# Exponential biases and softmax division computed on ScalarE in place of VectorE and GpSimd

## The chip, the core and the metric

The kernel runs on one core of a Trainium2 chip. The metric is device time in microseconds (us) of one execution. Five engines work side by side, each through its own list of instructions in a fixed order: TensorE (PE, with its weight loads as PEld), VectorE (DVE), ScalarE (ACT), GpSimd (POOL) and SyncE (SP), which issues the DMAs. An instruction waits, by semaphores, for what it reads and for the buffer that it writes, and everything behind it in the same list waits with it.

## The reference, cut to what matters

```python
proj = x @ w_in + b_in                       # x is layer-normed; 1024 x 1024 by 1024 x 3912
ya = spatial_gating(gelu(a_u), gelu(a_v), ...)
yb = chunk_band_attention(bq, bk, bv, b_rel)     # own chunk and 8 chunks before it
yc = dsa_attention(cq, ck, cv, iq, ik, iw, t5)   # top 256 keys by an indexer, then attention
ym = memory_attention(mq, km, vm)                # 256 memory tokens
mixed = concat([ya*silu(a_g), yb*silu(bg), yc*silu(cg), ym*silu(mg)])
out = layer_norm(ALPHA * x + (mixed @ w_out + b_out), ln_g, ln_b)

# in each of the three attentions, for every head and row:
p = softmax(s)          # exp(s - max(s)) / sum(exp(s - max(s)))
o = p @ v
```

All is float32. There are 1024 positions, and 4 heads of 64 in each group.

## The kernel before

Positions stand in 8 blocks of 128 (`rb`). Heads go in pairs (`odd` = 0, 1), so each attention has two pairs and 16 items (pair by block): M (memory, items of two blocks each), B (band) and C (top-k). Projections are three-part matmuls of 128x512 (`acc`), high and low halves of both operands.

An item of attention goes through these steps, which `mix_of` (B, C) and `mix_of_m` (M) write out. **scores**: PE makes `qk` in PSUM; DVE adds the bias and takes the row maximum (`mx`, or `nb` by a reduction in M); from it the bias of the exponential is made, `nb` = shift - max; ACT computes `sc` = exp(s + nb) and its row sum `rsum`. **turn**: `sc` is transposed to `pT`, for M and B by POOL (two float16 halves, lines 543 and 544) and a DMA transpose, for C by PE, ACT and DVE (`spread`). **values**: PE makes `pv`; `normalized` adds its three parts on DVE (`o`), takes the reciprocal `ri` of `rsum`, and multiplies `o` by `ri`. **close**: PE transposes `o` (bank `pt`), and DVE multiplies it by the gate into `mix`, which goes to DRAM or straight into the output projection.

The order of the work is written out by `weave`: parts of attention items alternate with pieces of projections ("fillers" on PE). A second filler is the search for the top-k threshold of C, bit by bit over 31 rounds: ACT counts three blocks (`jka`), DVE three others (`jk`), then DVE settles the bit in three small instructions (`bit`, `thr`, `cand`). It runs beside M and B; after it `masks` turns the scores into 0 or -1e30, and C reads them. The final order on each engine is set when the program is built, by a planner with costs of its own, so a changed instruction also moves others.

In `normalized`, `(V if kt in O_V else G)` sends the multiplication to DVE for `kt` 2 to 5 (B and C, 32 times) and to POOL for `kt` 6 (M, 16 times). `nb` is made by DVE, 8 times in M and 32 times in B and C.

Of the kernel before, what the change touches and what calls it, by code (L numbers as in the profile page):

```python
# [11 lines left out]
F32 = mybir.dt.float32  # L12
# [6 lines left out]
AF = mybir.ActivationFunctionType  # L19
ALU = mybir.AluOpType  # L20
# [4 lines left out]
P = 128  # L25
# [8 lines left out]
PSHIFT = 14.0 * math.log(2.0)  # L34
# [5 lines left out]
C0_FIRST, LATE = (0, 1, 6, 7, 5), "17 16 15 14 04 13 03 12 02 11 10"  # L40
HR = 2
WH = (0, 0)
O_V = (2, 3, 4, 5)
MHB = 2
LAG_O = 14
OB, LB = 400, 0
# [32 lines left out]
def tile_trunk(ctx, tc, x, mem, ln_in_g, ln_in_b, w_in, b_in, a_ln_g, a_ln_b, a_ws, a_bs,  # L79
               b_rel_rev, t5_table, w_mem, w_out, b_out, ln_g, ln_b, bucket1h, out):  # L80
    nc = tc.nc
    G, SP = nc.gpsimd, nc.sync
# [20 lines left out]
    PE, V, S = Engine(nc.tensor), Engine(nc.vector), Engine(nc.scalar)  # L103
# [9 lines left out]
    cp = ctx.enter_context(tc.tile_pool(name="cp", bufs=1))  # L113
# [6 lines left out]
    make_identity(nc, ident)  # L120
    mhalf = cp.tile([P, 1], F32, name="mhalf")
    V.memset(mhalf, -0.5)
    one = cp.tile([P, 1], BF16, name="one")
    S.activation(one, mhalf, AF.Copy, scale=-2.0)

# [11 lines left out]
    bias = cp.tile([P, 31], F32, name="bias")  # L137
# [33 lines left out]
    def small(shape, name, bufs=3):  # L171
        return gp.tile(list(shape), F32, tag=name, bufs=bufs, name=name)
# [81 lines left out]
    def two_heads(q, k, pieces):  # L254

        last = None
        for accs, c, n, qs, ks in pieces:
            for t, (x, y) in enumerate(((q[0], k[0]), (q[1], k[0]), (q[0], k[1]))):  # L260
                for odd in range(2):
                    rows = slice(64 * odd, 64 * odd + 64)
                    ins = PE.matmul(accs[odd][:, c:c + n], x[rows, qs:qs + P], y[rows, ks:ks + n],
                                    start=(t == 0), stop=(t == 2))
                    if last is not None:
                        tc.add_manual_dep(ins.ins, last.name, mybir.DependencyInfo(
                            mybir.DependencyClass.NoSync, mybir.DependencyReason.DATA), reason="in turn")
                    last = ins.ins

    def two_banks():  # L270
        return bank("qk"), bank("pt", "qk")
# [264 lines left out]
    def turned(sc, n):  # L536

        row, nb = sc.bitcast(F16), n // P  # L540
        both = 4 * n <= 2048
        high, rest = row[:, 2 * n:3 * n], row[:, 3 * n:4 * n] if both else row[:, :n]
        G.tensor_scalar(high, sc[:, :n], 1.0, 0.0, ALU.mult, ALU.add)  # L543
        G.tensor_sub(rest, sc[:, :n], high)  # L544
        t = gp.tile([P, 10, P], F16, tag="pT", bufs=TB, name="pT")
        if both:
            SP.dma_start_transpose(out=t[:, :2 * nb, :], in_=row[:, 2 * n:4 * n])
        else:
            SP.dma_start_transpose(out=t[:, :nb, :], in_=high)
            SP.dma_start_transpose(out=t[:, nb:2 * nb, :], in_=rest)  # L550
        return [t[:, j] for j in range(nb)], [t[:, nb + j] for j in range(nb)]
# [9 lines left out]
    def normalized(pv, rsum, kt):  # L561

        ri = small([P, 2], "ri")
        V.reciprocal(ri, rsum)
        o = small([P, 2, 64], "o", 2)
        done.append(V.tensor_reduce(o, pv[:, :384].rearrange("p (h t d) -> p h d t", h=2, t=3), AX.X, ALU.add).ins)
        (V if kt in O_V else G).tensor_mul(o, o, ri.unsqueeze(2).to_broadcast([P, 2, 64]))
        return o

    def gated(o, gate, dst):  # L570
# [97 lines left out]
    def mix_of_m(pair, rbs, q):  # L668

        d = {}  # L670

        def scores():
            accs = two_banks()
            two_heads(q, kmem[pair], [(accs, 256 * r, 256, rb * P, 0) for r, rb in enumerate(rbs)])
            nb = small([P, 2, 2], "nb2")
            for odd in range(2):
                V.tensor_reduce(nb[:, odd], accs[odd].rearrange("p (r n) -> p r n", r=2), AX.X, ALU.max)
            V.tensor_scalar(nb, nb, -0.125, PSHIFT, ALU.mult, ALU.add)
            for r in range(2):
                d["rsum", r] = small([P, 2], "rsum", 5)  # L680
                sc = gp.tile([P, 1024], F32, tag="S", bufs=SB, name="sc")
                for odd in range(2):
                    S.activation(sc[:, odd * 256:odd * 256 + 256], accs[odd][:, 256 * r:256 * r + 256], AF.Exp,
                                 bias=nb[:, odd, r:r + 1], scale=0.125, accum_out=d["rsum", r][:, odd:odd + 1])
                d["p", r] = turned(sc, 512)

        def values(r):
            ph, pl = d["p", r]
            pv = bank(("pv", "pt")[r], "pv")
            for odd in range(2):  # L690
                for i in range(2):
                    pv_mm(pv, odd, ph[2 * odd + i], pl[2 * odd + i], v3m[pair][:, i, odd], i == 0, i == 1)
            d["o", r] = normalized(pv, d["rsum", r], 6)

        def close():
            for r, rb in enumerate(rbs):
                t = small([P, P], "mix", 2)
                gated(d["o", r], gate_of(6 + pair, rb), t)
                store_mix(6 + pair, rb, t)

        return Item(scores, [], [lambda: values(0), lambda: values(1)], close)

    def mix_of(kt, rb, kb0, st, near, far_of, last):

        by_dma = kt < 4
        q, k, v3 = st
        nk = rb + 1 - kb0
        n = nk * P
        nfar = max(0, n - 256)
        chunks = list(range(0, nk, 4))  # L710
        d = {}

        def scores():
            d["rsum"] = small([P, 2], "rsum", 5)
            d["sc"] = [gp.tile([P, 1024], F32, tag="S", bufs=SB, name="sc") for _ in range(2)]
            mx = small([P, 2, 4], "mx")
            nr = [near(odd) for odd in range(2)]
            nmx = [0, 0]
            pieces = [(a, b) for a, b in pieces_of(n)]
            for group in [pieces] if by_dma else [[piece] for piece in pieces]:  # L720
                banks = [two_banks() if by_dma else (bank("qk"), bank("qk")) for _ in group]
                two_heads(q, k, [(accs, 0, b - a, rb * P, kb0 * P + a) for accs, (a, b) in zip(banks, group)])
                for (a, b), accs, odd in [(*x, odd) for x in zip(group, banks) for odd in range(2)]:
                    for lo, hi in ((a, min(b, nfar)), (max(a, nfar), b)):
                        if lo >= hi:
                            continue
                        other = far_of(lo, hi) if hi <= nfar else nr[odd][:, 256 - n + lo:256 - n + hi]
                        i = nmx[odd]
                        V.tensor_tensor_reduce(d["sc"][odd][:, lo:hi], accs[odd][:, lo - a:hi - a], other, 0.125,
                                               mx[:, odd, i - 1:i] if i else -3e38, ALU.add, ALU.max, mx[:, odd, i:i + 1])  # L730
                        nmx[odd] += 1
            nb = small([P, 2], "nb")
            V.tensor_scalar(nb, mx[:, :, nmx[0] - 1], -1.0, PSHIFT, ALU.mult, ALU.add)
            for odd in range(2):
                sc = d["sc"][odd]
                S.activation(sc[:, :n], sc[:, :n], AF.Exp, bias=nb[:, odd:odd + 1], accum_out=d["rsum"][:, odd:odd + 1])
                if by_dma:
                    d["p", odd] = turned(sc, n)

        def turn(odd, c):  # L740
            sc = d["sc"][odd]
            m = min(4, nk - c)
            pt = bank("pt")
            for j in range(m):
                PE.transpose(pt[:, j * P:(j + 1) * P], sc[:, (c + j) * P:(c + j + 1) * P], ident)
            d["p", odd, c] = spread(pt, m * P)

        def values(odd, c):
            if not odd and not c:
                d["pv"] = bank(("pv", "pt")[rb % 2 and by_dma], "pv")  # L750
            ph, pl = [part[c:] for part in d["p", odd]] if by_dma else d["p", odd, c]
            for j in range(min(4, nk - c)):
                pv_mm(d["pv"], odd, ph[j], pl[j], v3[:, kb0 + c + j, odd], c + j == 0, c + j == nk - 1)
            if odd and c == chunks[-1]:
                d["o"] = normalized(d["pv"], d["rsum"], kt)

        def close():
            last(lambda dst: gated(d["o"], gate_of(kt, rb), dst))

        steps = [(odd, c) for odd in range(2) for c in chunks]  # L760
        return [Item(scores, [] if by_dma else [lambda s=s: turn(*s) for s in steps], [lambda s=s: values(*s) for s in steps], close)]


# [615 lines left out]
```

## Time and profile before

| | us |
|---|---|
| median of 3 runs (684.84 to 686.62) | 686.62 |
| the profiled execution's own time | 686.82 |
| its span, first to last instruction | 685.0 |
| PE busy | 641.4 (94%) |
| DVE busy | 523.8 (76%) |
| ACT busy | 390.8 (57%) |
| POOL busy | 349.9 (51%) |

Between the span and the execution's own time lie 1.8 us. The granted TensorE clock was 0.989 over the span. M runs from about 200 to 330 us, B from 330 to 460, C from 460 to 640; then the output projection ends.

### The profile page before, as it was taken

What the parts mean: (1) busy time and instruction counts of PE and PEld (TensorE: products, weight loads), DVE (VectorE), ACT (ScalarE), POOL (GpSimd) and SP (SyncE); (2) the same over time, 40 slices, a digit from 0 to 9 for tenths busy, and PEclk for the clock granted to TensorE, in tenths of its full rate; (3) what the DMA queues carried; (4) which work ended last, traced back from release to release, by engine and by line L of the source; (5) the groups of instructions that cost most, each with busy time, mean ns of one, the idle gap of its engine ahead of it and who ended that gap; (6) DMA issues with size and microseconds to landing.
All of it is one profiled execution on the core that took longest, in us unless ns stands there. A gap on an engine that the chain in (4) does not pass through costs nothing.

```text
span 685.0 us, 11070 instructions
## 1 busy us (share of the span) xinstructions
PE 641.4 (94%) x3698; PEld 485.2 (71%) x3698; DVE 523.8 (76%) x1254; ACT 390.8 (57%) x801; POOL 349.9 (51%) x362
## 2 busy tenths in 40 slices
PE   4989999999999989989889999999999998999995
PEld 3957876677776767766567776777777766777785
DVE  6585256568767997899799889897578789789735
ACT  4665255456798887575878684445346554444210
POOL 3672311206347697575456436873222635559742
PEclk9999999999999999999999999999999999999998
DMA  9893511102236355346447333764002573143111
GB/s 276 233 303 100 174 44 32 31 17 80 60 108 126 75 124 135 74 106 153 89 106 140 79 93 78 149 124 114 31 19 80 170 230 108 69 140 139 66 61 62
DMA packets 121669, 75.30 MB, mean 110 GB/s; under 512 B 58976, under 2 KB 111500, under 8 KB 121612
## 3 DMA queue, kind: packets, MB, share of 16 engines
q1 hardware_dynamic: 121612, 74.59, 40.5%
q8 instruction: 29, 0.48, 0.3%
q14 instruction: 28, 0.23, 0.1%
HBM read 46.44 MB, written 17.64 MB: 94 GB/s over the span
## 4 chain that ended last, share of the span: by engine, by line
PE 48%; DVE 20%; ACT 11%; issue 5%; DMA 4%; POOL 3%; DVEq 0%; POOLq 0%; ACTq 0%; SPq 0%
PE acc L94 34%; PE qk L94 7%; ACT jka L94 5%; DVE jk L94 4%; PE pv L94 4%; PE pt L94 2%; ACT sc L94 2%; DVE nb L94 2%; DMA pT<-sc 2%; DVE thr L94 2%; DVE sc L94 1%; DVE o L94 1%; DVE bit L94 1%; DVE cand L94 1%; DVE score L94 1%
## 5 line engine op out<-in xcount | busy, mean ns | idle before, releaser
L94 PE MATMUL acc<-hTh,wblk 128*128 128x512 f32 (+1 forms) x960 | 320.9, 402 | 4.2 <-DVE iql L94 2.6
L94 PEld LDWEIGHTS acc<-hTh,wblk 128*128 128x128 f32 x960 | 178.3, 190 | 50.5 <-issue 8.0
L94 PE MATMUL acc<-hTl,wblk 128*128 128x512 f32 (+1 forms) x480 | 189.9, 396 | 0.0
L206 POOL TENSOR_TENSOR wblk<-raw,wblk 128x512 fp32r<-128x512 f32 x72 | 98.5, 1372 | 111.3 <-ACT wblk L94 109.3
L94 ACT ACTIVATE jka<-score,cand 128x768 int8<-128x768 f32 (+2 forms) x93 | 96.9, 1042 | 33.9 <-DVE cand L94 31.8
L94 PEld LDWEIGHTS acc<-hTl,wblk 128*128 128x128 f32 x480 | 90.9, 189 | 18.8 <-issue 2.8
L94 ACT ACTIVATE sc<-sc,nb 128x640 f32<-128x640 f32 (+7 forms) x64 | 46.6, 730 | 52.6 <-DVE nb L94 32.7
L94 PEld LDWEIGHTS <-pT 128*128 128x128 f16 x656 | 45.6, 99 | 38.0 <-issue 19.3
L94 DVE SCALAR_TENSOR_TENSOR score<-relu,iw,score 128x384 f32<-128x384 f32 (+5 forms) x42 | 43.8, 1059 | 22.4 <-ACT relu L94 20.6
L94 ACT ACTIVATE wblk<-raw 128x512 fp32r<-128x512 f32 x72 | 44.6, 628 | 27.4 <-PE acc L94 18.4
L94 PE MATMUL pv<-v,pT 128*128 128x192 bf16 (+1 forms) x528 | 55.0, 236 | 5.5 <-DMA pT<-sc 3.2
L544 POOL TENSOR_TENSOR sc<-sc 128x512 f16<-128x512 f32 (+4 forms) x48 | 55.5, 1164 | 1.7
L94 PE MATMUL acc<-woh,mh 128*128 128x512 f32 (+1 forms) x144 | 55.7, 387 | 0.1
L94 PE MATMUL acc<-wol,mh 128*128 128x512 f32 (+1 forms) x144 | 54.2, 376 | 0.0
L94 PE MATMUL acc<-woh,ml 128*128 128x512 f32 (+1 forms) x144 | 54.1, 378 | 0.0
L94 ACT ACTIVATE relu<-qk 128x384 f32<-128x384 f32 (+2 forms) x80 | 35.9, 530 | 22.5 <-PE qk L94 22.2
L543 POOL TENSOR_SCALAR sc<-sc 128x512 f16<-128x512 f32 (+4 forms) x48 | 32.8, 687 | 28.2 <-ACT sc L94 27.7
L94 ACT ACTIVATE pT<-pt 128x512 f16<-128x512 f32 (+3 forms) x48 | 22.1, 483 | 34.3 <-PE pt L94 34.2
L94 DVE TENSOR_SCALAR_CACHE_REDUCE jk<-planes,lo 128x384 bf16<-128x384 uint16 (+2 forms) x48 | 35.7, 743 | 0.9
L94 DVE TENSOR_SCALAR_CACHE_REDUCE jk<-planes,cand 128x384 bf16<-128x384 bf16 (+2 forms) x45 | 33.5, 744 | 1.0
L94 PE MATMUL qk<-kh,qh 64*128 64x384 f32 (+3 forms) x96 | 31.1, 418 | 1.8 <-DVE o L94 1.0
L94 PEld LDWEIGHTS acc<-woh,mh 128*128 128x128 f32 x144 | 27.2, 189 | 5.8 <-issue 1.1
(205 smaller groups left out, 1250.1 us busy)
## 6 DMA issues: line engine op xcount, KB each, us to landing
raw<-in_w_in SPq DMA_DIRECT2D x32, 512.0 KB, 3.9
xt<-in_x SPq DMA_DIRECT2D x8, 512.0 KB, 5.9
h_dram<-xt SPq DMA_DIRECT2D x8, 512.0 KB, 5.8
gate<-t SPq DMA_DIRECT2D x16, 256.0 KB, 2.0
rawo<-in_w_out SPq DMA_DIRECT2D x8, 512.0 KB, 4.6
hr<-h_dram SPq DMA_DIRECT2D x8, 512.0 KB, 5.0
out<-hr SPq DMA_DIRECT2D x7, 512.0 KB, 2.6
gate<-gate SPq DMA_DIRECT2D x48, 64.0 KB, 1.9
```

What stands on the lines that cost most here:

```text
L94: ins = op(*a, **k)
L206: G.tensor_sub(t[:, 1], r, f32(t[:, 0]))
L543: G.tensor_scalar(high, sc[:, :n], 1.0, 0.0, ALU.mult, ALU.add)
L544: G.tensor_sub(rest, sc[:, :n], high)
```

## The change

The 40 biases `nb` become ACT instructions (scale times input plus a constant column `shift1`), and each of the 48 multiplications by `ri` becomes two ACT instructions of 128x64, one per head, since ACT takes one scale per row. One memset on DVE makes the constant column.

```diff
+    shift1 = cp.tile([P, 1], F32, name="shift1")
+    V.memset(shift1, PSHIFT)
...
-        (V if kt in O_V else G).tensor_mul(o, o, ri.unsqueeze(2).to_broadcast([P, 2, 64]))
+        for odd in range(2):
+            S.activation(o[:, odd], o[:, odd], AF.Copy, scale=ri[:, odd:odd + 1])
...
-            V.tensor_scalar(nb, nb, -0.125, PSHIFT, ALU.mult, ALU.add)
+            S.activation(nb, nb, AF.Identity, bias=shift1, scale=-0.125)
...
-            V.tensor_scalar(nb, mx[:, :, nmx[0] - 1], -1.0, PSHIFT, ALU.mult, ALU.add)
+            S.activation(nb, mx[:, :, nmx[0] - 1], AF.Identity, bias=shift1, scale=-1.0)
```

The planner's order changes with it. Three places follow. In these rows the helper that records every operation is line 94 before and line 93 after.

On ACT in M, first pair: `jka` are the search's counts, `xh` and `t` take projections out of PSUM, `sc` are the exponentials. Before:

```order
L94 ACTIVATE jka,c<-score_682,cand 128x896
L94 ACTIVATE xh<-acc,hbias 128x512
L94 ACTIVATE wblk<-raw 128x512
L94 ACTIVATE jka,c<-score_683,cand 128x1024
L94 ACTIVATE t<-xh 128x512
L94 ACTIVATE t<-t 128x512
L94 ACTIVATE sc,rsum<-qk,nb_2319 128x256 x4
```

After, the same place:

```order
L93 ACTIVATE jka,c<-score_684,cand 128x896
L93 ACTIVATE o<-o,ri 128x64 x2
L93 ACTIVATE xh<-acc,hbias 128x512
L93 ACTIVATE wblk<-raw 128x512
L93 ACTIVATE jka,c<-score_685,cand 128x1024
L93 ACTIVATE o<-o,ri 128x64 x2
L93 ACTIVATE t<-xh 128x512
L93 ACTIVATE nb_2323<-nb_2323,shift_73 128x4
L93 ACTIVATE t<-t 128x512
L93 ACTIVATE o<-o,ri 128x64 x2
L93 ACTIVATE jka,c<-score_683,cand 128x768
L93 ACTIVATE sc,rsum<-qk,nb_2323 128x256 x4
```

Three pairs of multiplications and one bias now stand among the projections' and the search's instructions.

On DVE in B, first pair, around the scores of the fourth block (the first row with 384 far keys). Before:

```order
L94 TENSOR_TENSOR o<-o,ri 128x128
L94 SCALAR_TENSOR_TENSOR thr<-bit,thr 128x6
L94 TENSOR_SCALAR cand<-thr 128x6
L94 CAST lo<-cand 128x3
L94 TENSOR_SCALAR jk,c<-planes,lo 128x384
L94 RECIPROCAL ri<-rsum 128x2
L94 TENSOR_SCALAR jk,c<-planes,lo 128x512
L94 TENSOR_SCALAR jk,c<-planes,lo 128x640
L94 SCALAR_TENSOR_TENSOR ql<-acc,bias,qh 128x512
L94 TENSOR_TENSOR mix<-pt,gate 128x128
L94 ISA sc,mx<-qk,farB 128x384
```

After:

```order
L93 TENSOR_TENSOR bit<-c,bar 128x6
L93 SCALAR_TENSOR_TENSOR thr<-bit,thr 128x6
L93 TENSOR_SCALAR cand<-thr 128x6
L93 CAST lo<-cand 128x3
L93 TENSOR_SCALAR jk,c<-planes,lo 128x384
L93 TENSOR_SCALAR jk,c<-planes,lo 128x512
L93 TENSOR_REDUCE o<-pv 128x128
L93 TENSOR_TENSOR mix<-pt,gate 128x128
L93 RECIPROCAL ri<-rsum 128x2
L93 TENSOR_SCALAR jk,c<-planes,lo 128x640
L93 ISA sc,mx<-qk,farB 128x384
```

The multiplication is gone, and `mix` stands before the last count and before `ql`, which has moved behind the scores.

On ACT in C, around the exponentials of 768 keys; `pT` takes PE's transposes out of PSUM. Before:

```order
L94 ACTIVATE pT<-pt 128x384
L94 ACTIVATE sc,rsum<-sc,nb 128x768 x2
L94 ACTIVATE pT<-pt 128x512
L94 ACTIVATE pT<-pt 128x256
L94 ACTIVATE mh<-mix 128x128
```

After:

```order
L93 ACTIVATE pT<-pt 128x384
L93 ACTIVATE nb<-mx,shift_73 128x2
L93 ACTIVATE pT<-pt 128x512
L93 ACTIVATE sc,rsum<-sc,nb 128x768 x2
L93 ACTIVATE o<-o,ri 128x64 x2
L93 ACTIVATE pT<-pt 128x384
```

A bias stands ahead of the exponentials and a pair of multiplications between them and the next `pT`. Over the whole program ACT has 136 instructions more, DVE 71 fewer (with the memset) and POOL 16 fewer.

## Rows read from the trace of the kernel before

**Rows 1.** The page's first part: busy time, share of the span, instructions

```profile
PE 641.4 (94%) x3698; PEld 485.2 (71%) x3698; DVE 523.8 (76%) x1254; ACT 390.8 (57%) x801; POOL 349.9 (51%) x362
```

**Rows 2.** M, B, C: length, busy PE PEld DVE ACT POOL, clock, DMA, GB/s

```profile
200.00:330.00 130.00, 122.40 (x723) 93.64 (x723) 115.62 (x304) 98.16 (x218) 87.16 (x112) 0.99 0.48 110
330.00:460.00 130.00, 122.14 (x704) 87.47 (x703) 115.55 (x352) 85.53 (x174) 77.99 (x83) 0.97 0.50 104
460.00:640.00 180.00, 176.63 (x1073) 130.69 (x1072) 145.18 (x351) 85.02 (x184) 90.57 (x78) 1.00 0.34 109
```

**Rows 3.** Timeline of PE: start, us, instruction, idle time before it and its end

```profile
247.99 0.40 PE L94 MATMUL pv<-v3m,pT 128*128 128x192 bf16 x3 [2.38 <-DMA pT<-sc]
...
350.46 0.33 PE L94 MATMUL pt<-ident,o 128*128 128x128 f32 x1 [2.29 <-DVE mix L94]
...
385.08 0.33 PE L94 MATMUL pt<-ident,o 128*128 128x128 f32 x1 [0.75 <-DVE o L94]
...
426.11 0.38 PE L94 MATMUL qk<-kh,qh 64*128 64x256 f32 x1 [0.95 <-DVE o L94]
...
558.49 0.44 PE L94 MATMUL qk<-kh,qh 64*128 64x384 f32 x1 [0.82 <-DVE mx L94]
...
567.85 0.51 PE L94 MATMUL pv<-v,pT 128*128 128x128 bf16 x5 [1.47 <-DVE pT L94]
...
572.40 0.51 PE L94 MATMUL pv<-v,pT 128*128 128x128 bf16 x5 [0.85 <-DVE pT L94]
```

**Rows 4.** Groups of DVE and POOL: busy us, mean ns, idle before and releasers

```profile
L94 DVE TENSOR_TENSOR o<-o,ri 128x128 f32<-128x128 f32 x32 | 19.5, 610 | 0.2
...
L94 DVE TENSOR_SCALAR nb<-mx 128x2 f32<-128x2 f32 x32 | 10.9, 341 | 0.4
...
L94 DVE TENSOR_SCALAR nb<-nb 128x4 f32<-128x4 f32 x8 | 3.3, 412 | 0.0
...
L567 POOL TENSOR_TENSOR o<-o,ri 128x128 f32<-128x128 f32 x16 | 7.2, 452 | 11.8 <-DVE o L94 11.7
```

**Rows 5.** The same by tile: ns min/median/max, first and last start

```profile
L94 DVE TENSOR_SCALAR nb<-mx x32: 109/170/1337, 329.9 to 628.9; 128x2 f32<-128x2 f32 x32
...
L94 DVE TENSOR_TENSOR o<-o,ri x32: 278/374/2281, 344.2 to 643.1; 128x128 f32<-128x128 f32 x32
```

**Rows 6.** Timelines of DVE and of POOL at the long ones

```profile
237.40 1.26 DVE L94 TENSOR_SCALAR nb<-nb 128x4 f32<-128x4 f32 x1
...
342.82 0.69 DVE L94 TENSOR_SCALAR nb<-mx 128x2 f32<-128x2 f32 x1
...
422.00 0.87 DVE L94 TENSOR_TENSOR o<-o,ri 128x128 f32<-128x128 f32 x1
...
554.89 0.69 DVE L94 TENSOR_SCALAR nb<-mx 128x2 f32<-128x2 f32 x1
...
566.64 0.68 DVE L94 TENSOR_SCALAR nb<-mx 128x2 f32<-128x2 f32 x1
...
569.62 2.12 DVE L94 TENSOR_TENSOR o<-o,ri 128x128 f32<-128x128 f32 x1
...
569.21 2.39 POOL L1239 TENSOR_TENSOR hr<-hr,bo 128x1024 f32<-128x1024 f32 x1
```

**Rows 7.** One stretch of 3.4 us, 1.8 us after the wait at 350.46

```profile
352.30:355.70 3.40, 3.40 (x12) 2.28 (x11) 3.29 (x13) 2.80 (x7) 1.74 (x2) 0.50 0.56 124
```

**Rows 8.** Groups of ACT with the nearest shapes, and the search's largest count

```profile
L94 ACT ACTIVATE jka<-score,cand 128x1024 int8<-128x1024 f32 x31 | 35.6, 1147 | 0.4
...
L94 ACT ACTIVATE iw<-iwt 128x64 f32<-128x64 f32 x1 | 0.2, 224 | 0.1
...
L94 ACT ACTIVATE one<-mhalf 128x1 bf16<-128x1 f32 x1 | 0.2, 205 | 0.0
```

**Rows 9.** ACT's last step on the mask of block 6; DVE's first use

```profile
433.37 0.94 ACT L94 ACTIVATE score<-score 128x896 f32<-128x896 f32 x1
...
480.88 0.56 DVE L94 CUSTOM_DVE_ANT_0 sc<-qk,score 128x384 f32<-128x384 f32 x1 [1.31 <-PE qk L94]
```

More of the change, by code (lines that the diff above doesn't have):

```diff
@@ L42 @@
 WH = (0, 0)
-O_V = (2, 3, 4, 5)
 MHB = 2
```

## The prediction

> **What bounds the kernel now.** I read the page's busy times first: PE is busy 94% of the span, no other engine over 76% [rows 1]. The end is set by PE, so the change can only pay or cost through PE's waits, and the question is where PE waits for what the change touches. The windows by stage answer the first half: PE is idle 130 - 122.4 = 7.6 us in M, 130 - 122.1 = 7.9 us in B and 180 - 176.6 = 3.4 us in C [rows 2], 18.9 us together. The work before 200 us and after 640 us holds nothing that the change edits. So 18.9 us of idle, and what low clock adds, is the whole field for a gain; a loss has no such ceiling.
>
> In the same windows DVE is the fullest of the others: 115.6 of 130 us in M and in B, 145.2 of 180 in C. ACT has 98.2, 85.5 and 85.0, so it has room in B and C and little in M, and POOL 87.2, 78.0 and 90.6 [rows 2].
>
> The timeline of PE then says what ended its waits [rows 3]. The seven waits that I use are 2.38, 2.29, 0.75, 0.95, 0.82, 1.47 and 0.85 us, 9.5 of the 18.9. One ended with a transposing DMA, all others with an instruction of DVE.
>
> The groups show the odd thing that decides my forecast. The multiplication of 128x128 on DVE takes 0.61 us in the mean, and a bias of two columns 0.34 us [rows 4]; their minimum and median are 0.28 and 0.37, and 0.11 and 0.17, but their maxima are 2.28 and 1.34 us [rows 5]. In the timelines a long one lies beside a POOL instruction and ends with it: the multiplication from 569.62 to 571.74 beside POOL's addition from 569.21 to 571.60 [rows 6]. These small DVE instructions stand still while POOL works, and all behind them on DVE with them.
>
> **What is taken off.** DVE loses 32 multiplications (19.5 us), 32 biases (10.9) and 8 biases (3.3), 33.7 us of recorded time; POOL loses 16 multiplications, 7.2 us and the 11.8 us that it sat idle ahead of them [rows 4]. Most of that is beside PE's work and worth nothing. What counts are PE's waits with a long one of these in the DVE list ahead of their releaser [rows 3, 6]:
>
> - 247.99, for a DMA transpose. Its exponentials waited for the bias at 237.40, 1.26 us long. On ACT it is 0.2, so the chain starts 1.05 us earlier.
> - 350.46, for `mix`. Ahead of it DVE had the bias at 342.82 (0.69) and two multiplications, at least 0.28 each [rows 5]; the second of them heads the order shown above. 1.25 us.
> - 426.11, for `o`. The multiplication at 422.00 (0.87) and a bias stood ahead of that sum; 0.87 alone covers nearly the whole wait. 0.9 us.
> - 558.49, for `mx`. The bias at 554.89 was 0.69 long, its exponentials and what followed came late. 0.69 - 0.2 = 0.5 us.
> - 567.85, for `pT`. The bias at 566.64 stood right ahead of it: 0.7 us.
> - 572.40, for `pT`. The multiplication at 569.62 blocked it for 2.12 us: the whole wait, 0.85 us.
>
> That is 5.25 us. The clock adds to it: from 352.3 to 355.7, 1.8 us after the wait of 2.29 us, the granted clock is 0.50, the 1.2 GHz level of the two, while PE is busy throughout [rows 7]. PE does there what takes it 1.7 us at 2.4 GHz, so the stretch costs 1.7 us. With that wait cut by 1.25 us I expect this dip to go: 6.95 us in all.
>
> **What is added.** ACT has no such row before. The nearest are an activation of 128x64 at 0.224 us and one of 128x1 at 0.205 us [rows 8]; both write little, and I take them as they are. 96 x 0.224 + 40 x 0.205 = 21.5 + 8.2 = 29.7 us on ACT, of which 32 x 0.224 + 8 x 0.205 = 8.8 us in M. From below the bound is nothing (they fit into idle time), and ACT is idle 31.8 us of M, 44.5 of B and 95.0 of C [rows 2]. From above: `o` now takes 0.45 us instead of 0.28, and may stand behind a count of 1.15 us that is just running [rows 8]. At ACT's busy share of about 0.65 and half a count on average that is 0.4 + 0.17, some 0.55 us for each of the 48, 26 us if PE waited for every one. It does not: PE has other matmuls ahead of the transposes. The wait at 385.08 [rows 3] is the pattern that gets worse: it ended with the multiplication itself. I take 5 to 6 of 48 as coupled so closely, 3.0 us. The bias costs no new wait between engines: before, DVE's `mx` went to a DVE bias and that to ACT; now `mx` goes to ACT, and the exponential follows on the same engine.
>
> The rules of the Trainium skill, "ScalarE: Activation LUTs", section "Rules for kernel authors", speak against the change: additions and multiplications belong on VectorE, and an activation is to be budgeted at about 0.3 us and 0.83 ns an element. An estimate by it is 96 x 0.353 + 40 x 0.30 = 46 us on ACT, 13.7 of them in M, against 29.7 and 8.8 by the rows; the sum itself would lose perhaps 2 us of its gain. The nearest rows of this trace are lower than that budget; a 64-column activation from SBUF is in no row yet.
>
> The search keeps its rounds, but in the new order its last counts and the masks come later. That is hidden: block 6's mask is done at 434.3 and first read at 480.88 [rows 9], 46.6 us of slack. If the search slipped beyond that, each further microsecond would be one on PE.
>
> **The sum.** -5.25 - 1.7 + 3.0 = -3.95 us on the profiled execution's 686.8 us, which agrees with the median of the runs (686.62): **682.8 us**.
>
> **The rivals.**
>
> *The same waits, elsewhere.* The planner writes a new order on every engine. PE is 94% busy, POOL still makes DVE's remaining small instructions stand still, and new places of 1 to 2 us can replace old ones. For it: only half of PE's idle time is in the waits above. Against it: the blocked time on DVE really is shorter. It gives a gain of 2 us or less, 685 to 688.5.
>
> *ACT becomes the late engine in M (slower).* Before, POOL sat idle for 11.8 us ahead of its 16 multiplications, because DVE's sum `o` was not there [rows 4]. Now ACT's list stands in that place, and behind it stand `xh`, which frees the projections' PSUM banks, and the exponentials, as the order of M shows. ACT in M would have 98.2 + 8.8 + 11.8 = 118.8 of 130 us taken, before the waits that it already has, which fill its 31.8 us of idle time. If these 20.6 us cannot be absorbed at all, M grows by 20.6; if half can, by about 10. It decides once PE waits for ACT by 4 us more than the 3.0 that the sum already holds. Against it: ACT's present waits are in good part for the search, which can slip. At half it gives 682.8 + 10.3 = 693 us, at the full price 703. By the budget of the Trainium skill's "ScalarE: Activation LUTs" this case would cost 4.9 us more in M.
>
> *No gain from the moved biases.* Should an activation of 128x2 take longer than the 0.34 us that DVE's takes in the mean, the biases are no gain; at 0.205 us for 128x1 that is unlikely, and it falls under the first rival.
>
> **Chances.** A difference of 0.3%, 2.1 us, is about what measurement can tell here. Forecast (faster by 2.1 to 12 us): 0.51. Same waits elsewhere: 0.22. ACT late: 0.27. The range: the most that the forecast's mechanism could give is all 15.5 us of idle in M and B, 671; I take 675, where 11.5 of it is gone, and 694 above, just over ACT's case at half. Its own range for the likeliest case is 676 to 684.5.
>
> **What the new profile would show.** Right: DVE's busy time down by some 30 us, POOL's by 7; the activations `o` near 0.22 and `nb` near 0.2 us with no long maximum; PE's idle time in M to C below 18.9 us, with no waits for `pT` behind a multiplication; fewer stretches at clock 0.5. Wrong: waits of PE for `xh`, `t`, or exponentials in M; ACT idle ahead of `o` by 10 us and more; `jka` ending past 434 us so that C waits for its masks; new PE waits of about 2 us with a clock dip behind each.

## The result and the profile after

The changed kernel takes 680.43 us in the median (679.7 to 681.43, 4 runs) against 686.61 us (684.84 to 686.62, 4 runs). The ratio is 0.9917, with a 95% interval of 0.9897 to 0.9938, so it is faster by 6.2 us, where 3.95 were forecast. (Here and below a ratio compares all executions with those of the kernel before on the same chip; it need not be the quotient of the two medians.) The profiled execution took 681.43 us, 5.4 less than the one before.

The page's first part of the changed kernel:

```profile
PE 642.8 (95%) x3698; PEld 486.7 (72%) x3698; DVE 493.5 (73%) x1183; ACT 421.6 (62%) x937; POOL 342.2 (50%) x346
```

The windows of M, B and C of the changed kernel, with the columns of [rows 2]:

```profile
200.00:330.00 130.00, 123.29 (x717) 94.63 (x716) 113.58 (x296) 107.32 (x260) 81.71 (x100) 0.97 0.47 112
330.00:460.00 130.00, 127.85 (x741) 90.99 (x739) 109.71 (x329) 98.73 (x222) 83.48 (x79) 1.00 0.54 108
460.00:640.00 180.00, 177.72 (x1072) 133.03 (x1072) 130.31 (x327) 96.37 (x236) 86.59 (x79) 0.99 0.33 110
```

Against [rows 1], DVE is down by 30.3 us, POOL by 7.7, and ACT up by 30.8. PE is idle 6.7 us in M, 2.2 in B and 2.3 in C. Against the 7.6, 7.9 and 3.4 of [rows 2], 18.9 us became 11.1, and most of that is B. Over the whole span PE's idle time fell by 6.8 us (43.6 to 36.8), and its busy time rose by 1.4.

The timeline of PE marks the same places, the first scores of B and the first transpose of C. Before:

```profile
322.23 0.33 PE L94 MATMUL qk<-kh,qh 64*128 64x128 f32 x1
...
474.56 0.33 PE L94 MATMUL pt<-ident,sc 128*128 128x128 f32 x1
```

After:

```profile
323.70 0.49 PE L93 MATMUL qk<-kh,qh 64*128 64x128 f32 x2
...
470.44 0.27 PE L93 MATMUL pt<-ident,sc 128*128 128x128 f32 x1
```

B starts 1.5 us later, and from its first scores to the first transpose of C it is 146.7 us in place of 152.3, which is 5.6 less.

What ended PE's waits between 200 and 640 us (total us, times, longest), in the view of waits. Before, the first six groups:

```profile
PE pv L94 <- DMA pT<-sc: 6.4, 5, 2.4
PE pv L94 <- DVE pT L94: 2.3, 2, 1.5
PE pt L94 <- DVE mix L94: 2.3, 1, 2.3
PE qk L94 <- DVE mix L94: 2.0, 1, 2.0
PE pv L94 <- DVE o L94: 1.6, 1, 1.6
PE qk L94 <- DVE o L94: 1.0, 1, 1.0
```

After, all groups from 0.4 us:

```profile
PE pv L93 <- DVE amix L93: 4.7, 1, 4.7
PE pv L93 <- DMA pT<-sc: 2.2, 4, 1.0
PE qk L93 <- DVE mx L93: 1.7, 1, 1.7
PE pt L93 <- DVE mx L93: 1.0, 1, 1.0
PE acc L93 <- ACT t L93: 0.5, 1, 0.5
PE acc L93 <- DVE ml L93: 0.4, 1, 0.4
PE pt L93 <- DVE ri L93: 0.4, 1, 0.4
```

The groups of waits for `pT` on DVE, for `mix` and for `o` are gone, and those for the DMA transpose are down by 4.2 us. One wait of 4.7 us is new. Its place, in the timelines of PE, DVE and POOL of the changed kernel:

```profile
307.44 1.92 PE L93 MATMUL pv<-v3m,pT 128*128 128x192 bf16 x13 [4.71 <-DVE amix L93]
...
304.23 1.64 DVE L93 TENSOR_TENSOR planes<-jk,score 128x512 uint16<-128x512 uint16 x1
305.90 0.88 DVE L93 TENSOR_SCALAR_CACHE_REDUCE jk<-planes,hi 128x640 bf16<-128x640 bf16 x1
...
306.70 0.69 DVE L93 TENSOR_TENSOR amix<-pm,atab 128x512 f32<-128x512 f32 x1
...
304.00 1.32 POOL L207 TENSOR_TENSOR wblk<-raw,wblk 128x512 fp32r<-128x512 f32 x1
305.28 1.60 POOL L545 TENSOR_TENSOR sc<-sc 128x512 f16<-128x512 f32 x1
```

`amix` belongs to the first branch (the spatial gating). It reads `pm`, which lies in a bank of the kind `pt`, and half of the `pv` of M use that kind too. In DVE's list five instructions of the search (and two short reads of an accumulator) stand between the end of `pm`'s matmuls (301.67) and `amix`, and one of these, `planes` with two inputs, lasted 1.64 us beside POOL; the same instruction took 0.83 us in the kernel before.

The granted clock, in windows. Before, two stretches besides that of [rows 7]:

```profile
294.30:297.70 3.40, 3.40 (x20) 2.81 (x17) 3.40 (x9) 3.28 (x6) 2.60 (x5) 0.50 0.16 48
338.60:342.00 3.40, 3.40 (x13) 2.21 (x13) 3.33 (x15) 2.57 (x5) 1.60 (x3) 0.51 0.46 88
```

After:

```profile
306.20:313.00 6.80, 5.56 (x27) 4.87 (x27) 6.80 (x16) 2.49 (x7) 3.71 (x6) 0.50 0.73 178
524.60:528.00 3.40, 3.40 (x9) 2.69 (x9) 3.40 (x10) 1.85 (x4) 1.15 (x1) 0.50 0.97 298
```

Between 200 and 640 us it is 10.2 us at the 1.2 GHz level in both kernels. The two stretches of B are gone, and the long one of M lies at the end of the new wait. The profiled execution of the changed kernel has two more of 3.4 us, at 16 and 122 us, ahead of the first `nb` or `o`. They are not the change's: the execution of `all_on_vector` (below), in which no `o` or `nb` is on ACT, has them too, and that of `dve_one_input`, which is the changed kernel with spare instructions, has not.

The new instructions on ACT, by tile (ns min/median/max):

```profile
L93 ACT ACTIVATE o<-o,ri x96: 330/336/367, 221.4 to 637.8; 128x64 f32<-128x64 f32 x96
...
L93 ACT ACTIVATE nb<-mx,shift x32: 281/297/298, 327.0 to 623.2; 128x2 f32<-128x2 f32 x32
```

None is ever long.

### The profile page after: what moved, and what is told of

Its sections match the earlier page's. It is cut to its first block, busy times and chain, and to the rows that moved or that the text cites. A ratio compares the mean times of both kernels' runs of the same rounds, so it can differ in the third digit from the quotient of the medians.

```text
span 679.6 us, 11076 instructions
## 1 busy us (share of the span) xinstructions
PE 642.8 (95%) x3698; PEld 486.7 (72%) x3698; DVE 493.5 (73%) x1183; ACT 421.6 (62%) x937; POOL 342.2 (50%) x346
## 5 line engine op out<-in xcount | busy, mean ns | idle before, releaser
L207 POOL TENSOR_TENSOR wblk<-raw,wblk 128x512 fp32r<-128x512 f32 x72 | 101.0, 1407 | 124.3 <-ACT wblk L93 119.0
L545 POOL TENSOR_TENSOR sc<-sc 128x512 f16<-128x512 f32 (+4 forms) x48 | 58.0, 1213 | 2.3
L93 PE MATMUL acc<-wol,mh 128*128 128x512 f32 (+1 forms) x144 | 54.3, 377 | 0.0
L544 POOL TENSOR_SCALAR sc<-sc 128x512 f16<-128x512 f32 (+4 forms) x48 | 31.2, 652 | 34.8 <-ACT sc L93 32.8
L93 ACT ACTIVATE o<-o,ri 128x64 f32<-128x64 f32 x96 | 27.9, 340 | 12.4 <-DVE o L93 12.2
L93 PE MATMUL qk<-kh,qh 64*128 64x384 f32 (+3 forms) x96 | 32.7, 417 | 1.9 <-DVE mx L93 1.7
```

What stands on the lines that cost most here:

```text
L93: ins = op(*a, **k)
L207: G.tensor_sub(t[:, 1], r, f32(t[:, 0]))
```

## The experiments

The theory: small DVE instructions with two inputs (and `nb`, which has one) stand still while POOL works, and what stands behind them on DVE comes late for PE. The rivals: DVE simply has less to do; only a part of the change pays; the gain is a lucky order. No edit changes what is computed; the spare instructions of three kernels write a tile that nobody reads. The planner orders each kernel anew, so an edit also moves other instructions, unless it is said that it doesn't.

**One half at a time.** `nb_only` keeps the two activations `nb` of the change and leaves `o` as before; `o_only` the reverse.

> Only the 40 biases on ScalarE; the 48 multiplications as before. If the gain comes from VectorE's list, freed of small instructions that stand still while GpSimd works, the terms of the sum that hang on a bias remain (1.05 + 0.7 + 0.5 + 0.7 us, some 3 us) and the time is about 683.5 us. If the gain is only the planner's new order, the halves need not add up to the whole, and either half can be slower than before (687 us or more).

> Only the 48 multiplications on ScalarE (96 instructions); the biases as before. By the first theory the terms that hang on a multiplication remain (0.55 + 0.9 + 0.85 us, and perhaps a clock dip of 1.7), less the price of ScalarE's queue (3.0 us predicted, less if PE is not coupled so closely): 683 to 687 us. If this alone gives nearly all of the gain (681 us), the biases were not worth their terms, and the price of ScalarE's queue was about nothing.

`nb_only`: 688.34 us (685.49 to 693.73, 12 runs), ratio 1.0016 [0.9988, 1.0043]. `o_only`: 686.07 (682.82 to 690.13, 12), 0.9981 [0.9961, 1.0001]. Neither half is a gain that can be told from none. For `nb_only` that contradicts the first theory's 683.5 us and lies where the expectation put a mere change of order (687 or more); `o_only` lies within its 683 to 687. The groups of DVE may be part of the reason. `nb_only`, the multiplications that stayed there, and `o_only`, the biases that stayed:

```profile
L94 DVE TENSOR_TENSOR o<-o,ri 128x128 f32<-128x128 f32 x32 | 23.9, 747 | 0.3
```

```profile
L94 DVE TENSOR_SCALAR nb<-mx 128x2 f32<-128x2 f32 x32 | 15.5, 484 | 0.3
```

In [rows 4] they were 19.5 us (610 ns) and 10.9 (341). The kind that stays takes 4.4 or 4.6 us more than before. In `nb_only` that leaves DVE 3.3 us less busy than before (520.5); in `o_only`, though, it is 21.8 us less (502.0), so there this is not the whole reason. In `nb_only` the wait for `amix` is there as well, 5.7 us. In `o_only`, whose profiled execution is the longest of its 12, one close waited 2.29 us for ACT:

```profile
317.16 0.33 PE L94 MATMUL pt<-ident,o 128*128 128x128 f32 x1 [2.29 <-ACT o L94]
```

**Two inputs or one, at the same place.** Two spare instructions behind each `ri` of the changed kernel, 96 in all. The first kernel has the upper pair of lines, the second the lower:

```diff
+        for _ in range(2):
+            V.tensor_mul(small([P, 2], "spare", 2), ri, ri)
...
+        for _ in range(2):
+            V.reciprocal(small([P, 2], "spare", 2), ri)
```

> The changed kernel, and for each of the 48 multiplications two spare VectorE multiplications of two columns by themselves (ri by ri, two inputs from SBUF), whose result nobody reads. They hang on VectorE's own reciprocal alone. If VectorE's list with stalled small instructions is what costs time, the spare ones have maxima of 1 to 2.4 us, VectorE is 20 to 30 us busier, and half or more of the gain is lost: 683 to 686 us. If only order and latency matter, 680 to 682 us.

> The same with two spare reciprocals of two columns (one input) in place of the spare multiplications. The first theory, by its mechanism of two inputs that stand still beside GpSimd: each stays near 0.16 us, VectorE is some 15 us busier, and less is lost than with two inputs: 681 to 683 us. If just the number of VectorE's instructions counts, this loses the same as the one with two inputs.

Two inputs: 693.97 us (691.4 to 695.62, 6), 1.0094 [1.0065, 1.0124], 8 us above the 683 to 686 that were expected: the whole gain is lost, and more. One input: 683.14 (680.09 to 687.04, 12), 0.9946 [0.9922, 0.9971]. By their traces the two programs have the same order on DVE, ACT and POOL, and on PE all but 25 of the 3698 matmuls stand at the same place, so the 10.8 us between them are hardly the planner's. The spare instructions, by tile, first kernel and second:

```profile
L93 DVE TENSOR_TENSOR spare<-ri x96: 145/160/2241, 213.5 to 638.7; 128x2 f32<-128x2 f32 x96
```

```profile
L93 DVE RECIPROCAL spare<-ri x96: 137/150/167, 211.1 to 622.7; 128x2 f32<-128x2 f32 x96
```

Their minimum and median are alike; the maximum is not. The groups have 33.7 and 10.9 us. (By its busy time DVE has only 7.3 us more with one input than in the changed kernel, where 15 were expected.) The 2.31 us of two of them, in the timeline of DVE, lie beside POOL's addition:

```profile
597.76 2.31 DVE L93 TENSOR_TENSOR spare<-ri 128x2 f32<-128x2 f32 x2
...
597.56 2.41 POOL L1243 TENSOR_TENSOR hr<-hr,bo 128x1024 f32<-128x1024 f32 x1
```

The two traces also differ in the clock. Between 200 and 640 us it is 0.50 to 0.51 in three stretches with two inputs, and in one with one input:

```profile
310.00:316.60 6.60, 5.43 (x26) 4.86 (x26) 6.60 (x16) 1.77 (x5) 3.04 (x5) 0.50 0.62 148
422.50:425.90 3.40, 3.08 (x11) 2.47 (x12) 3.40 (x12) 1.95 (x4) 1.94 (x2) 0.51 0.45 98
569.40:576.00 6.60, 6.42 (x30) 4.67 (x30) 4.34 (x19) 3.90 (x10) 5.15 (x5) 0.50 0.23 76
```

```profile
303.70:310.30 6.60, 4.33 (x24) 3.98 (x24) 6.57 (x14) 3.52 (x9) 4.72 (x7) 0.50 0.66 140
```

PE's busy time is 647.1 us against 641.9, so 5.2 of the 13.2 us between the two spans (691.6 and 678.4) are longer work, and 8.0 are idle time. But this overstates the clock's part: the profiled execution with one input (680.22 us) is one of the two shortest of its 12, and the one with two inputs has the two early stretches, at 16 and 122 us, ahead of the first spare instruction. Over all executions the median of the granted clock is 0.984 with two inputs and 0.985 with one, which is worth under 1 us by my estimate. So little of the 10.8 us is clock.

The Trainium skill, "SBUF — State Buffer", section "Who interferes with whom", says that a DVE instruction with two inputs from SBUF contends with a GpSimd instruction that reads SBUF, that one with a single input outside the two-port modes does not, and that ScalarE waits for nobody. The trace agrees in each: 2241 ns against 167, and 367 at most on ACT.

**More on DVE, more on ACT.** `all_on_vector` takes the kernel before and moves POOL's 16 multiplications to DVE; `scalar_load` gives the kernel before 96 spare instructions on ACT.

```diff
-O_V = (2, 3, 4, 5)
+O_V = (2, 3, 4, 5, 6)
...
+        for odd in range(2):
+            S.activation(small([P, 2], "spare", 2), ri, AF.Copy, scale=ri[:, odd:odd + 1])
```

> The kernel before, with the 16 multiplications of M on VectorE too instead of GpSimd. If stalled two-input instructions on VectorE cost time, 16 more of them cost 1 to 4 us: 688 to 691 us. If what counted was GpSimd's blocked list (11.8 us idle ahead of them), it is faster than before: 682 to 685 us.

> The kernel before, with 96 spare ScalarE instructions of two columns (ri times ri, unused) behind each reciprocal. ScalarE gets some 25 us more, without relief for VectorE. My theory: ScalarE's price is small, 0 to 3 us (687 to 690 us). The rival, that a fuller ScalarE queue is dear, which the change pays and VectorE's relief hides: 692 us or more.

`all_on_vector`: 690.02 us (688.1 to 695.15, 12), 1.0056 [1.0034, 1.0077]. The window of M says where; PE is idle 13.75 us there:

```profile
200.00:330.00 130.00, 116.25 (x696) 88.31 (x694) 118.34 (x310) 95.35 (x213) 77.35 (x95) 1.00 0.46 105
```

So 16 such instructions more on DVE cost PE 6.2 us of idle time in M with this order, though POOL is rid of them.

`scalar_load`: 692.21 (684.97 to 694.4, 12), 1.0054 [1.0024, 1.0084]. Four of its executions lie at 685.0 to 688.3 and eight at 691.3 to 694.4. The granted clock over the span goes with it: 0.989 to 0.992 in the four, 0.983 to 0.984 in seven of the eight and 0.988 in the longest. That is worth some 5 of the 7 us by my estimate; why it differs was not found. The profiled one (692.1) has 6.4 us of idle time in C, and clock 0.97 in B and in C. The median lies where the rival was expected (692 or more), the ratio makes it 3.7 us, a little over the theory's 3. So load on ACT is not free here in general, and that the change pays such a price, hidden by what DVE gains, is not excluded.

**The new wait.** `pm` in another kind of bank, in the changed kernel and in `nb_only`:

```diff
-        pm = bank("pt", "pm")
+        pm = bank("qk", "pm")
```

> The changed kernel, with the small PSUM tile pm of the gating group in the qk banks instead of the pt banks. In the changed kernel PE waits 4.71 us for a pt bank that amix still reads behind the search's instructions on VectorE, and then has 6.8 us at half clock. If that wait belongs to the planner's order and not to ScalarE's part of the work, it goes with the bank: 4.7 us and some 3.4 us of clock, 673 to 676 us. If the wait only shows that VectorE or ScalarE is behind at this point, another wait takes its place: 679 to 681 us.

> Only the biases on ScalarE, and pm in the qk banks. With the biases alone the time was that of before, and its trace has the wait for amix (5.68 us, and 6.8 us at half clock). If that wait hid the gain of the biases, this comes to 678 to 682 us; if the biases have no gain, it stays at 685 us or more.

On the changed kernel: 681.72 us (678.9 to 683.26, 6), 0.9914 [0.989, 0.9937], which is no different from the change alone. On `nb_only`: 685.81 (680.45 to 688.57, 12), 0.9984 [0.9961, 1.0007], against its 1.0016. PE no longer waits for `amix` in either. Others have come. The waits of the first:

```profile
PE pv L93 <- DMA pT<-sc: 3.4, 4, 1.4
PE qk L93 <- DVE mx L93: 2.1, 2, 1.8
PE vt L93 <- ACT vT L93: 1.6, 1, 1.6
PE pv L93 <- DVE vr L93: 1.6, 1, 1.6
PE pt L93 <- DVE mix L93: 1.2, 1, 1.2
```

With the order that the planner then came to, the end of a wait of 4.7 us was worth nothing, as the second case of the expectation had it. The biases alone have no gain with the other bank either.

**Forms that don't stand still, on DVE.** The same arithmetic on DVE in a form that also adds up its results: one input from SBUF for each head of `o`, and two steps for `nb`.

```diff
+            V.tensor_scalar(o[:, odd], o[:, odd], ri[:, odd:odd + 1], None, ALU.mult, ALU.add, accum_out=small([P, 1], "spare", 2))
...
+            for op, x, src in ((ALU.mult, -1.0, mx[:, :, nmx[0] - 1]), (ALU.add, PSHIFT, nb)):
+                V.tensor_scalar(nb, src, x, None, op, ALU.add, accum_out=small([P, 1], "spare", 2))
```

`vector_forms` has both on DVE, `mixed_forms` has `o` in this form and `nb` on ACT, and `nb_form_o_scalar` `nb` in this form and `o` on ACT. The changed kernel ran again beside the first two.

> Nothing goes to ScalarE. The multiplications (all 48, two of 128x64 each) and the biases (two steps each) stay on VectorE, but in the form that also writes its sum, with a scalar per row, which is the form of the search's counts; the counts never stood still in the trace. If the cost is that two-input and plain scalar instructions on VectorE stand still beside GpSimd, these take 0.1 to 0.25 us each with no long maximum, and the time falls below before though VectorE has more instructions than before: 679 to 684 us. If the gain needs the work off VectorE, the added instructions make it slower than before: 687 to 692 us.

> Biases on ScalarE as in the changed kernel, the 48 multiplications on VectorE in the form that does not stand still (96 of 128x64). By the stall theory VectorE's stalled time is as low as in the changed kernel, and ScalarE is spared 32 us: 677 to 681 us. If VectorE's plain occupancy counts as much as its stalls, 683 to 687 us.

> The multiplications stay on ScalarE as in the changed kernel, and the biases go back to VectorE in the accumulating form that was never seen to stand still (two steps for each, 80 instructions of 0.15 us and as many reads of the accumulator of 0.08 us, some 18 us on VectorE). If what counts is that neither of the two stands still beside GpSimd, on whichever engine it is, this is as fast as the kernel with the two places exchanged (683.3): 681 to 685 us, ratio 0.992 to 0.997. If what counts is how much work VectorE is relieved of, it lies near the kernel with only the multiplications moved, 685 to 688 us, since VectorE is then as full as it is there (502 us). In either case nb has no maximum over 0.2 us.

> The changed kernel beside the two others on the same chip, for a direct comparison: 680 to 682 us by any theory.

| | median us | ratio | DVE busy us | ACT busy us |
|---|---|---|---|---|
| `changed_again` | 681.31 (6) | 0.9922 [0.9896, 0.9947] | 493.6 | 421.6 |
| `mixed_forms` | 683.3 (6) | 0.9932 [0.9907, 0.9957] | 514.0 | 399.0 |
| `vector_forms` | 685.57 (12) | 0.9976 [0.9959, 0.9993] | 519.5 | 389.7 |
| `nb_form_o_scalar` | 685.09 (12) | 0.9993 [0.9968, 1.0018] | 505.1 | 412.9 |

The multiplications in `vector_forms` and the first step of the biases in `nb_form_o_scalar`, by tile:

```profile
L94 DVE TENSOR_SCALAR_CACHE_REDUCE o<-o,ri x96: 248/274/280, 224.0 to 640.5; 128x64 f32<-128x64 f32 x96
...
L93 DVE TENSOR_SCALAR_CACHE_REDUCE nb<-mx x32: 96/149/157, 329.1 to 625.2; 128x2 f32<-128x2 f32 x32
```

They never pass 280 and 157 ns, where those of [rows 5] reached 2281 and 1337. With DVE nearly as full as before (514.0 and 519.5 us against 523.8), `mixed_forms` gains 0.7% and `vector_forms` 0.2%. But the last row speaks against a simple account: there nothing of `o` or `nb` stands still either, DVE has 18.7 us less than before, and no gain can be told (680.5 to 690.1 in 12 runs). So DVE's busy time alone does not order these kernels, and the absence of long `o` and `nb` doesn't either. The expectations don't decide it: 683.3 lies in the range for the case that DVE's plain occupancy counts as much (683 to 687), and 685.57 lies between the two ranges set for it.

One count can be made over all the traces: the recorded time of DVE's instructions above the shortest that the same operation on the same tile and shape took in any of the kernels, wherever that is over 0.3 us. By this estimate DVE stood still for 70.4 us before and 48.5 in the changed kernel; for 69.5 in `nb_only` and 56.1 in `o_only`; for 50.5, 51.9 and 54.3 in `mixed_forms`, `vector_forms` and `nb_form_o_scalar`; and for 70.1 and 48.2 with the spare instructions of two inputs and of one. In `nb_only` nearly all of the standing still is there as before, in other instructions. Over all 14 kernels the count goes with the ratios a little more closely than DVE's busy time does (correlation 0.89 against 0.82). That supports the theory, but it is one execution of each, and each has an order of its own.

## Why the prediction was right, and where it was not

**The mechanism** is shown; that the gain comes from it is shown in part. Small two-input DVE instructions stand still beside POOL, and PE pays for it: with the order kept, 96 of them cost 10.8 us more than 96 with one input. That the multiplications and the biases stand still too is in [rows 5, 6]. But the bias has one input, and no run tests its form with the order kept.

**The gain of 5.25 us in six waits** was mis-sized. The sum took six single waits from the timeline [rows 3] and cut each. The groups of waits show that `mix`, `o` and DVE's `pT` went altogether, and with them waits that I hadn't listed, such as 2.0 us of `qk` for `mix` and 1.6 of `pv` for `o`. Against it stands the new wait of 4.7 us. PE's idle time in M to C fell by 7.8 us net. Nor do the terms stand for themselves, as the sum has it: those of the biases, some 3 us, gave no gain in `nb_only`. That the total of 3.95 came near the measured 6.2 is in part luck, since the clock's 1.7 us were not won, the 3.0 us for ACT are not seen, and the waits that I hadn't listed stand against one that I hadn't foreseen.

**The clock's 1.7 us** were wrong in the sum. The dip of [rows 7] did go, with the wait ahead of it, as the step said. But the new wait brought one of 6.8 us, and C one of 3.4, so the total from M to C stayed at 10.2 us.

**The 3.0 us for ACT's queue** were too many, as far as waits show it. PE's only wait of 0.4 us or more that ended with ACT is 0.5 us, for a projection's `t`. The pattern of the wait at 385.08 did not get worse; no wait for `o` is left. `o_only` shows that it can: 2.29 us for one `o`.

**ACT's prices** were too low. I took 0.224 and 0.205 us from the nearest rows, and they are 0.336 and 0.297 (medians). The budget of the Trainium skill's "ScalarE: Activation LUTs", section "Rules for kernel authors", 0.353 and 0.30 by my estimate, was the better price by far. ACT's busy time still rose by only 30.8 us, near the 29.7 of the sum, and that is luck: by the medians the new instructions last 44 us, but neighbours on ACT overlap, so that the two of a pair start some 0.24 us apart and last 0.34. The advice of the same section, multiplications on VectorE, is not borne out by the whole change, which gained with them on ACT; by themselves they gained nothing there (`o_only`).

**The rivals.** The first, the same waits elsewhere, came in part: it is the 4.7 us for `amix` behind a `planes` that stood still beside POOL. It may also tell of the halves: 1.0016 and 0.9981 alone, 0.9917 together, and the kind that stayed took up 4.4 or 4.6 us more on DVE. The second, ACT late in M, did not come about. ACT sat idle 12.2 us ahead of `o` for DVE's sum, which is one of the signs that I had named, but only 4.8 of that in M, where POOL had 11.8 [rows 4], and in M its idle time for the search's `cand` fell by 8.5 us. ACT's group over the whole kernel, its waits in M (200 to 330 us) before, and after:

```profile
L93 ACT ACTIVATE o<-o,ri 128x64 f32<-128x64 f32 x96 | 27.9, 340 | 12.4 <-DVE o L93 12.2
...
ACT jka L94 <- DVE cand L94: 20.4, 11, 5.1
...
ACT jka L93 <- DVE cand L93: 11.9, 7, 5.3
ACT o L93 <- DVE o L93: 4.8, 5, 1.4
```

So the search gave way, as the argument against this rival had it, and PE hardly waited for what stood behind (0.5 us, for `t`). The third's condition did not come about, an activation `nb` takes 0.297 us and DVE's mean was 0.341; its outcome, no gain from the biases by themselves, did in `nb_only`, where `o` stood still for longer.

**The search** did not come late. Block 6's mask has its last step at 433.95 in place of 433.37 [rows 9], and PE has no wait for `score`. But the slack of 46.6 us was misread: 480.88 is DVE's first use, and POOL reads the mask long before it, 1.3 us after it was done:

```profile
435.61 1.48 POOL L1146 TENSOR_TENSOR comb<-score,nearC 128x256 f32<-128x256 f32 x2
```

**What stays open.** How much of the 6.2 us is less standing still and how much is the order that the planner came to. Both halves together give some 7 us more than their sum by the medians (+1.7 and -0.6 us), and every one of these kernels has an order of its own. Only the pair with the spare instructions had it fixed, and that pair shows the mechanism, not the share. That `nb_form_o_scalar` has no gain is not explained; it is the strongest sign that the order has a part in it. No run here beat the changed kernel by what can be measured.

## What to carry to other kernels

Read the minimum, median and maximum of small VectorE instructions: if the maximum is many times the median (6 to 14 times here) and the long ones lie beside GpSimd, the instruction is standing still, and its mean isn't its price. Removing one kind need not pay, since the kind that stays took up 4.4 to 4.6 us here. A form that does not stand still, on the same engine, can be a second remedy (0.7% in one kernel here, 0.2% and nothing in two others). Of PE's waits count the groups by releaser, not a chosen few, and expect a new one: removing the longest (4.7 us) gained nothing.

## What was unexpected of the hardware

A two-column multiplication of 0.16 us in the median can last 2.24 us beside POOL, and 96 of them, worth 33.7 us on DVE, cost the kernel 10.8 us more than 96 reciprocals of the same shape (150 ns in the median, 167 at most). And 96 activations of two columns in the kernel before left some executions at 685 us and put others at 692, with the same program; the granted clock was 0.989 to 0.992 in the former and 0.983 to 0.988 in the latter.
